# Sums of the down weights formed in DRAM by accumulating transfers, and four more lower parts prepared ahead, in a one-layer transformer kernel

## The chip, the cores and the metric

The kernel runs on one core of a Trainium2 chip. The metric is device microseconds (us) of that core for one execution, lower is better. Engines are named as the profile names them: PE (matrix multiply), DVE (vector), ACT (scalar activation), POOL (GpSimd), SP (the queue that issues nearly all transfers).

## What is computed

One layer on 512 rows of 1024 floats, all in float32: a gated feed-forward part, a mixer with two kinds of attention, and a second feed-forward part, each between two norms.

```python
def swiglu(h, w_gate, w_up, w_down):
    return (jax.nn.silu(h @ w_gate) * (h @ w_up)) @ w_down
...
h = swiglu(rms_norm(x, ff1_norm_pre[l]), ff1_w_gate[l], ff1_w_up[l], ff1_w_down[l])
x = x + 0.5 * rms_norm(h, ff1_norm_post[l])
h = hybrid_mixer(rms_norm(x, mix_norm_pre[l]), w_in[l], ...)      # diff attention and sparse attention
x = x + rms_norm(h, mix_norm_post[l])
h = swiglu(rms_norm(x, ff2_norm_pre[l]), ff2_w_gate[l], ff2_w_up[l], ff2_w_down[l])
x = x + 0.5 * rms_norm(h, ff2_norm_post[l])
```

The gate and up weights are 1024 x 2816, the down weights 2816 x 1024, `w_in` is 1024 x 2840.

## The kernel before, in words

**Precision.** A float32 product is made of three PE products of a shorter float type: each operand is split into an upper part (a cast, by ACT or DVE) and a lower part (the operand minus its upper part, by DVE), and PE adds upper x upper, upper x lower and lower x upper. So every weight tile that PE reads costs one cast and one DVE subtraction (`split`, L398 to L412; L404 is the cast, L407 the subtraction).

**Fewer products.** The products of both feed-forward parts are 2 x 2 block products made with seven block products in place of eight, numbered `m` = 1 to 7. Four of the seven use sums of weight blocks. In the gate and up half (names `ff1q..`, `ff1a`, `ff1b`, `ff1c`, line L664 on PE) these sums are DVE additions (L525). The quads `c` = 0 to 10 of gate (`e` = 0) and up (`e` = 1) weights come in two transfers each (`j` = 0, 1) of 512 KB, written (c, e, j) here; even c go through 4 `raw` tiles, odd c through 5 others (L332 issues them).

**The down half** (`ff1y`, L808 and L768 on PE) runs after it. `down_products` walks `m` in the order 1, 5, 6, 2, 7, 4, 3. `factor` (called for each m) fetches, for each of four row groups q, the weight blocks into `raw` tiles (`rawff1d`), adds them on DVE where m wants a sum (`add`, L601), and splits the result into `ff1dw<m><q>h` and `ff1dw<m><q>l`. For m = 5 the sum is block 00 + block 01, for 6 that sum + block 11, for 4 again that sum + block 10, for 7 block 01 + block 11. The activations' side is split likewise into `ff1dl`. The second feed-forward part does the same under `ff2` names.

**Lower parts ahead.** Twelve of the 512 KB pieces of `w_in` (three groups of columns, from 512, 0 and 1024) have their lower parts made early: `ahead` loads a piece (`pre`), casts it on ACT (L352), subtracts on DVE (L353) and stores the lower part to DRAM (`low`, L354); the projection later loads it instead of subtracting (L380). The four pieces of the columns from 1536 (`wp22` to `wp25`, the queries `qn`) are split when they are used.

**What sets the order.** Every step is recorded as an `Op` with a guessed cost and put in order by a planner (`Graph.order`), which simulates the engines with room in the tile pools (`ROOM`, `CAPS`) and picks on each engine the ready step with the highest level plus a number from the table `BIAS`. Each engine then runs its list strictly in that order. All transfers but a few are in SP's one list: an SP entry that waits holds back every transfer behind it.

Of the kernel before, what the change touches and what calls it, by code (L numbers as in the profile page):

```python
# [18 lines left out]
P = 128  # L19
# [34 lines left out]
    "ACT:fh>fdl": 5.6, "ACT:fh>fdl@ACT": -68.3, "ACT:fh>fdl@DVE": -0.3, "ACT:fh>fhh": 16.2, "ACT:fh>fhh@DVE": -182,
    "ACT:fhr>fhh": -138.7, "ACT:fhr>fhh@ACT": 20, "ACT:fhr>fhh@DVE": -242.2, "ACT:fp_>fp_": 134.6,
    "ACT:fqu>fqw": 937.3, "ACT:fqv>fqw": 100.3, "ACT:fy>fdp": 44, "ACT:gr>gh": 1255.8, "ACT:htk>hTk": -17.2,
    "ACT:htv>hTv": -173.1, "ACT:k__t>kT": 25.7, "ACT:ls>ls": 40.7, "ACT:n_nm>n_l": 46.2, "ACT:n_t>n_th": 116.1,
    "ACT:n_t>xa": -94.5, "ACT:n_t>xaf0": -210.9, "ACT:n_t>xaf1": 11.9, "ACT:n_t>xb": 327.4, "ACT:n_t>xc": 49.3,
    "ACT:n_t>xcf1": -137.4, "ACT:nc_pc>nc_pc": -84.3, "ACT:nc_t>nc_h": 25.6, "ACT:oN>oTn": 59.7,
    "ACT:oN>oTn@ACT": -12.7, "ACT:oN>oTn@DVE": -5.8, "ACT:pa>cd": 32.4, "ACT:pa>k__dup": 127.2, "ACT:pa>v": -109.4,  # L60
    "ACT:pb>k__dup": 21.1, "ACT:pb>v": 19.9, "ACT:pk>dkd": -48.9, "ACT:pre>pre": 191.7, "ACT:pre>preh": 0.9,
    "ACT:pv>dv": -90.4, "ACT:qTd_>qTd": 7.3, "ACT:qTn_>qTn": -44.2, "ACT:qd>qdd": 5.5, "ACT:qn>qdn": 23.6,
    "ACT:raw>wp": -2.3, "ACT:raw>wp@ACT": 20.1, "ACT:raw>wp@DVE": -4, "ACT:rawff1d>fdwh": 18.3,
    "ACT:rawff1d>fdwh@ACT": -113.1, "ACT:rawff1d>fdwh@DVE": -13.4, "ACT:rawff1q>fqw": 3.5, "ACT:rawff2d>fdwh": -25.9,
    "ACT:rawff2d>fdwh@ACT": -55.9, "ACT:rawff2d>fdwh@DVE": -67.9, "ACT:rawff2q>fqw": -83.9, "ACT:uk>uk": -98.6,
    "ACT:uv>uv": -22.7, "ACT:wrk>wk": 42.2, "ACT:wrv>wv": -96.2, "ACT:xaf0>xa": 12.9, "ACT:xaf0>xa@ACT": -0.2,
    "ACT:xaf0>xa@DVE": -99.7, "ACT:xaf1>xa": 5.7, "ACT:xaf1>xa@ACT": -49.8, "ACT:xaf1>xa@DVE": 21.3,
    "ACT:xcf0>xc": -165.4, "ACT:xcf0>xc@ACT": -92.6, "ACT:xcf1>xc": -156.2, "ACT:xcf1>xc@DVE": 213.5,
    "ACT:xi>n_ss": -6, "ACT:xj>n_ss": -11.3, "ACT:xm>n_ss": 95.1, "ACT:xrv>Xv": 189.3, "ACT:xrv>Xv@ACT": -72.1,
    "ACT:xrv>Xv@DVE": -45, "ACT:z>o_ss": 13.3, "DVE:acc>oN": -6, "DVE:cd_t>kc": 8, "DVE:ck>kcT": -19,  # L70
    "DVE:cmask>cmb": -77, "DVE:cmk>uk": -91.8, "DVE:cmv>uv": 103.6, "DVE:cv>vc": -15, "DVE:d>d_p": -21.7,
    "DVE:d_acc>o": 29.2, "DVE:d_r>d_p": 40.3, "DVE:d_t>d_th": 53.2, "DVE:dkt>dk": 7.8, "DVE:dl>d_r": -29.5,
    "DVE:dl>do_r": -0.4, "DVE:dmask>dmb": 5.2, "DVE:do_rr>o": 39.5, "DVE:do_t>oTd": 3.5, "DVE:fb>fhs": -65.9,
    "DVE:fb>fp_": 8.2, "DVE:fc>fhs": 24.7, "DVE:fc>fp_": 0.5, "DVE:fc__sg>fh": 23.8, "DVE:fd>fhs": -37.7,
    "DVE:fdp>fy": 12, "DVE:fdq>fy": 19.9, "DVE:fdr>fy": 1.9, "DVE:fds>fdl": 1.5, "DVE:fdu>fdwl": 62.2,
    "DVE:fh>fdl": -29.3, "DVE:fh>fds": 14.2, "DVE:fh>fh": 11.2, "DVE:fh>fhl": 92.5, "DVE:fh>fhl@DVE": 9.3,
    "DVE:fh>fhl@POOL": 1.1, "DVE:fhr>fhl": 156.6, "DVE:fp_>fh": 53.9, "DVE:fp_>fhs": 43.6, "DVE:fp_>fp_": 39.7,
    "DVE:fqu>fqw": 1255.3, "DVE:fqv>fqw": -218.6, "DVE:fy>fdr": 4.2, "DVE:gr>gh": 1080.8, "DVE:gsub>gsub": -24.1,
    "DVE:htk>hTk": -33.2, "DVE:htv>hTv": -60.3, "DVE:k__t>kT": 46.9, "DVE:lp>ls": 49, "DVE:ls>nlam": 0.6,
    "DVE:n>n_p": 4.9, "DVE:n_cf>n_p": 22, "DVE:n_cf>n_p@DVE": -1.2, "DVE:n_cf>n_p@POOL": 14, "DVE:n_l>n_cf": -8.8,  # L80
    "DVE:n_t>n_th": -9.5, "DVE:n_t>xa": -96.2, "DVE:n_t>xb": 0.5, "DVE:n_t>xc": 1861.1, "DVE:nc>nc_pc": -160.3,
    "DVE:nc_t>nc_h": -18.1, "DVE:oN>oTn@DVE": 0.7, "DVE:o_yg>xi": 22.6, "DVE:o_yg>xm": -74.8, "DVE:o_yg>xo": 136.3,
    "DVE:pa>k__dup": -42.2, "DVE:pb>k__dup": 6.6, "DVE:pb>v": 5.1, "DVE:pek>xrk": 235.1, "DVE:pev>xrv": 8.5,
# [1469 lines left out]
```

## Time and profile before

| | |
|---|---|
| runs | 999.89, 1001.97, 1004.66 us |
| median | 1001.97 us |
| the profiled execution | 1003.56 us, its span 1001.8 us |
| PE busy | 983.5 us (98%), DVE 882.9 us (88%), ACT 589.5 us (59%), POOL 32.3 us (3%) |
| bytes moved | 154.39 MB; the transfers of SP's queue take 45.4% of the 16 DMA engines' time |

Stages on the time axis of the profiled span: start and first norm to about 30 us, gate and up of the first part to 242 us, its down half to about 360 us, projections and compression to 425 us, attention to 590 us, output projection to 655 us, gate and up of the second part to 885 us, its down half to the end. A matmul that waits inside PE's pipeline is still counted as busy, so the count of matmuls in a stretch says more than the busy share.

### The profile page before, as it was taken

How to read it: one execution, taken by the hardware profiler on the slowest of the kernel's cores; microseconds unless marked ns; L12 is line 12 of the kernel's file. 1: busy time of each engine (PE TensorE's matmuls, PEld its weight loads, DVE VectorE, ACT ScalarE, POOL GpSimd, SP SyncE). 2: the span in 40 equal slices, each digit the busy share in tenths (PEclk: the TensorE clock that was granted, in tenths of full speed). 3: DMA queues.
4: the chain of work that ended last, by engine and by line, in shares of the span. 5: the costliest groups of instructions: out<-in, count | busy, mean ns of one | idle time of the engine just before them, and what ended most of it. 6: DMA issues, size and time to landing. Idle time of an engine off the chain costs nothing.

```text
span 1001.8 us, 17153 instructions
## 1 busy us (share of the span) xinstructions
PE 983.5 (98%) x6504; PEld 893.9 (89%) x6504; DVE 882.9 (88%) x1612; ACT 589.5 (59%) x1143; POOL 32.3 (3%) x68
## 2 busy tenths in 40 slices
PE   8999999999899999999999999999999999999997
PEld 7999999999688888888888888899999999988786
DVE  7999999999999687977887799899989998999984
ACT  8655555665454475577877677776554555545542
POOL 1000000000000030000000001310000000000001
PEclk9999999999899999999999999999999999999999
DMA  9126554556768754540403142361334231287752
GB/s 336 64 86 179 168 178 127 164 173 242 258 222 293 244 179 147 190 168 1 169 1 110 59 167 86 106 232 53 137 106 135 68 136 43 86 281 244 231 210 84
DMA packets 100420, 154.39 MB, mean 154 GB/s; under 512 B 11121, under 2 KB 61553, under 8 KB 100338
## 3 DMA queue, kind: packets, MB, share of 16 engines
q1 hardware_dynamic: 100338, 153.30, 45.4%
q8 instruction: 51, 0.84, 0.3%
q14 instruction: 31, 0.25, 0.1%
HBM read 137.55 MB, written 15.73 MB: 153 GB/s over the span
## 4 chain that ended last, share of the span: by engine, by line
PE 85%; DVE 6%; DMA 4%; ACT 2%; issue 1%; SPq 0%; POOL 0%; DVEq 0%; POOLq 0%; ACTq 0%
PE ff2b L664 9%; PE ff1b L664 9%; PE ff1y L808 7%; PE ff2c L664 6%; PE ff1c L664 6%; PE ff2a L664 6%; PE ff1a L664 6%; PE ff2y L808 5%; PE z L1410 4%; PE ff2y L768 3%; PE ff1y L768 2%; PE n_t L1306 2%; DMA rawff2d<-ff_w_down 1%; PE n L1190 1%; PE acc L398 1%
## 5 line engine op out<-in xcount | busy, mean ns | idle before, releaser
L1203 ACT ACTIVATE n_p<-n_p,n_nm 128x128 f32<-128x128 f32 (+3 forms) x64 | 35.3, 554 | 9.0 <-DVE n_nm L1201 8.6
L1201 DVE CUSTOM_DVE_ANT_0 n_p<-n,dmb 128x128 f32<-128x128 f32 (+3 forms) x64 | 28.3, 486 | 5.9 <-PE n L1191 5.6
L407 DVE TENSOR_TENSOR n_th<-n_t,n_th 128x512 fp32r<-128x512 f32 x40 | 25.8, 684 | 6.6 <-ACT n_th L404 6.4
L404 ACT CAST n_th<-n_t 128x512 fp32r<-128x512 f32 x40 | 21.6, 594 | 7.0 <-PE n_t L1306 6.7
L439 POOL TENSOR_SCALAR o_ms<-o_ss 128x1 f32<-128x1 f32 x12 | 4.0, 335 | 664.6 <-ACT junk L447 664.5
L691 ACT ACTIVATE ff1p<-ff1p 128x256 f32<-128x256 f32 x30 | 12.5, 418 | 19.2 <-DVE ff1p L703 19.2
L691 ACT ACTIVATE ff2p<-ff2p 128x256 f32<-128x256 f32 x30 | 12.5, 417 | 16.5 <-DVE ff2p L703 15.7
L1203 ACT ACTIVATE d_p<-d_p,d_nm 128x128 f32<-128x128 f32 (+3 forms) x32 | 17.7, 556 | 5.7 <-DVE d_nm L1201 5.5
L1306 PEld LDWEIGHTS n_t<-ident,n_p 128*128 128x128 f32 x160 | 18.6, 140 | 2.5
L1306 PE MATMUL n_t<-ident,n_p 128*128 128x128 f32 x160 | 20.7, 272 | 0.0
L703 DVE TENSOR_TENSOR ff2p<-ff2p,ff2b 128x512 f32<-128x512 f32 x30 | 20.4, 681 | 0.3 <-PE ff2b L664 0.3
L1190 PE MATMUL n<-kT,qTn 128*128 128x128 f32 (+3 forms) x64 | 20.4, 335 | 0.0
L703 DVE TENSOR_TENSOR ff1p<-ff1p,ff1b 128x512 f32<-128x512 f32 x30 | 20.4, 680 | 0.0
L1191 PE MATMUL n<-kT,qTn 128*128 128x128 f32 (+3 forms) x64 | 19.6, 321 | 0.0
L569 DVE TENSOR_TENSOR o_yg<-ff2y,g_ff_norm_post 128x512 f32<-128x512 f32 x8 | 5.5, 689 | 14.3 <-ACT junk L447 14.3
L447 ACT ACTIVATE junk<-ff2y 128x512 bf16<-128x512 f32 x8 | 4.8, 597 | 21.3 <-PE ff2y L768 21.3
L398 PE MATMUL acc<-n_th,v 128*64 128x512 f32 x40 | 16.1, 402 | 0.0
L1201 DVE CUSTOM_DVE_ANT_0 d_p<-d,dmb 128x128 f32<-128x128 f32 (+3 forms) x32 | 14.7, 486 | 1.2 <-PE d L1191 1.2
L399 PE MATMUL acc<-n_th,v 128*128 128x512 f32 x40 | 15.7, 393 | 0.0
L470 PE MATMUL n_t<-ident,n_xn 128*128 128x128 f32 x96 | 13.3, 286 | 1.2 <-DVE n_xn L463 1.2
L703 DVE TENSOR_TENSOR ff2p<-ff2c,ff2p 128x512 f32<-128x512 f32 x20 | 13.8, 688 | 0.3
L1296 DVE TENSOR_SCALAR n_p<-n_p,n_cf 128x128 f32<-128x128 f32 (+3 forms) x42 | 13.8, 380 | 0.3
(1831 smaller groups left out, 3562.6 us busy)
## 6 DMA issues: line engine op xcount, KB each, us to landing
rawff1d<-ff_w_down SPq DMA_DIRECT2D x36, 512.0 KB, 4.7
rawff2d<-ff_w_down SPq DMA_DIRECT2D x36, 512.0 KB, 5.0
rawff1q<-ff_w_gate SPq DMA_DIRECT2D x22, 512.0 KB, 5.8
rawff1q<-ff_w_up SPq DMA_DIRECT2D x22, 512.0 KB, 4.3
rawff2q<-ff_w_gate SPq DMA_DIRECT2D x22, 512.0 KB, 5.1
rawff2q<-ff_w_up SPq DMA_DIRECT2D x22, 512.0 KB, 4.2
raw<-w_in SPq DMA_DIRECT2D x20, 512.0 KB, 4.5
pre<-w_in SPq DMA_DIRECT2D x12, 512.0 KB, 4.2
```

The source lines that it names most:

```text
L398: nc.tensor.matmul(oh, vh, b(1), start=False, stop=False)
L407: V.tensor_sub(lo(), src(), f32(hi()))
L664: nc.tensor.matmul(o, T[k][:, s, i * P:(i + 1) * P], T[xm][:, r, i, :], start=start and e + i + s + r == 0, stop=stop and i == 3 and s == ...
L691: op("ACT", act(256), lambda: A.activation(T[sg][:, :256], T[sg][:, :256], AF.Silu), w=[sg])
L703: op("DVE", dve(512), lambda: fn(T[out], T[x], T[y]), r=[k for k in (x, y) if k != out], w=[out])
L768: nc.tensor.matmul(T[f"{f}y{t}{j}"], T[a[s]][:, sl], wp[i](r)[:, j, :], start=start and s + r == 0, stop=c == rest[-1] and s == 1, skip_gr ...
L808: nc.tensor.matmul(T[ys[u]], T[k][:, s, q % 2 * 2 + n, u * P:(u + 1) * P], T[ws[r]][:, n, :], start=m in (1, 5, 6) and q + n + s + r == 0, ...
L1190: nc.tensor.matmul(T[b][:, :L], qt[:, 0, h, :], k()[:, :L], start=True, stop=False)
L1201: op("DVE", dve(L), lambda: V.tensor_tensor_reduce(T[p][:, :L], T[b][:, :L], T["dmb"][:, S - L:], -1.0, 3e38, ALU.add, ALU.min, T[nm][:, 0 ...
L1203: op("ACT", act(L, 0.22), lambda: A.activation(T[p][:, :L], T[p][:, :L], AF.Exp, bias=T[nm][:, 0:1], scale=-1.0, accum_out=T[l][:, col:col ...
L1306: nc.tensor.transpose(T[bt][:, h * P:(h + 1) * P], T[p[h]][:, kb * P:(kb + 1) * P], ident)
L1410: nc.tensor.matmul(T[y[j]], T[f"oT{t}{'nd'[k < 4]}{s}"][:, k % 4, :], wp[wo[k]](r)[:, j, :], start=k == 4 and s + r == 0, stop=k == 3 and ...
```

## The change

It does four things.

1. `down_products` gets a second argument, the load after which it may begin (quad transfer 12, which is (3, 0, 0), of each part). For each q and each m of 5, 6, 7 and 4 it makes a 512 KB tile in DRAM (`ff1sum..`): SP copies one operand into it, DRAM to DRAM (L647 of the changed kernel), and POOL issues a transfer that adds the second operand onto it (L649). That is 16 copies and 16 accumulating transfers for each feed-forward part. The first operand of 6 is the finished sum 5, that of 4 the finished sum 6. POOL's sixteen stand in the order q by q, 5, 6, 7, 4.
2. `factor` now loads one `raw` tile for each m and q, from the weights or from the sum, and splits it. The 16 DVE additions of each part are gone, and the tiles `du` with them; 28 `rawff1d` loads stand where 36 stood.
3. The columns from 1536 join the pieces whose lower parts are made ahead: 16 in place of 12, with 1536 first.
4. `BIAS` is replaced by a longer table, entries of the form `...@engine` now count for every step, and the norm ahead of the first part has the names `na` (rows 0, 1) and `nb` (rows 2, 3).

```diff
-    "ACT:acc>ol": -8.4, "ACT:ck>kcT": 114.7, "ACT:cmk>prek": -4, "ACT:cmv>prev": -52.6, "ACT:cv>vc": -40.9,
...
+    "ACT:acc>ol": -15.1, "ACT:cd_t>kc@ACT": -26871.7, "ACT:ck>kcT": 75.7, "ACT:cmv>prev": -52.6,
...
-                    heapq.heappush(ready[e], (-o.level - (BIAS.get(f"{kind_of(o)}@{e}", 0.0) if len(o.eng) > 1 else 0.0), o.n, o))
+                    heapq.heappush(ready[e], (-o.level - BIAS.get(f"{kind_of(o)}@{e}", 0.0), o.n, o))
...
-    def down_products(f):
...
-        def add(dst, a, b, r):
-            op("DVE", dve(1024), lambda: V.tensor_add(T[dst], T[a], T[b]), r=[k for k in r if k != dst], w=[dst], port=True, chain="sum")
...
+    def down_products(f, after):
+
+
+        def src(q, kh, jh):
+            r0 = (2 * SPILL + 8 * kh + 2 * q) * P
+            return io[f"{f}_w_down"][0, r0:r0 + 2 * P, jh * 512:(jh + 1) * 512].rearrange("(k p) b -> p k b", p=P)
+
+        sums = {}
         for q in range(4):
-            new(f"{f}du{q}", ("M", "m_u"), [P, 1024])
+            for m, a, b in ((5, (0, 0), (0, 1)), (6, 5, (1, 1)), (7, (0, 1), (1, 1)), (4, 6, (1, 0))):
+                k = f"{f}sum{m}{q}"
+                d = sums[m, q] = dram.tile([P, 2, 512], F32, name=k)
+                first = sums[a, q] if isinstance(a, int) else src(q, *a)
+                op("SP", 1.46, lambda d=d, first=first: nc.sync.dma_start(d, first), r=[f"{f}sum{a}{q}"] if isinstance(a, int) else [],
+                   w=[k], after=after)
+                op("POOL", 7.0, lambda d=d, b=src(q, *b): nc.gpsimd.dma_start(d, b, accum_op=ALU.add), w=[k], after=after, chain="acc")
...
-    def factor(f, m, raw, add):
+    def factor(f, m, sums, src):
         for q in range(4):
-            u = f"{f}du{q}"
-            if m == 5:
-                a, b = raw(q, 0, 0, m), raw(q, 0, 1, m)
-                add(u, a, b, [a, b])
...
+            u = new(f"raw{f}d{m}{q}", "raw", [P, 1024])
+            part = {1: (0, 0), 2: (1, 0), 3: (1, 1)}.get(m)
+            a, r = (src(q, *part), []) if part else (sums[m, q], [f"{f}sum{m}{q}"])
+            v = lambda u=u: T[u].rearrange("p (a b) -> p a b", a=2)
+            pdma.append(op("SP", 1.46, lambda v=v, a=a: nc.sync.dma_start(v(), a), r=r, w=[u], chain="dma"))
...
-    dp1 = down_products("ff1")
+    dp1 = down_products("ff1", [qdma[12]])
...
-    low_i = {c: [ahead(*in_rows(c, 512, j)) for j in range(4)] for c in (512, 0, 1024)}
+    low_i = {c: [ahead(*in_rows(c, 512, j)) for j in range(4)] for c in (1536, 512, 0, 1024)}
...
-    w = in_pieces(1536, 512)
+    w = in_pieces(1536, 512, low_i[1536])
...
-    dp2 = down_products("ff2")
+    dp2 = down_products("ff2", [qdma[56]])
```

DVE at the start of the first down half, before: `ff1du` are the sums, `ff1dw5.`, `ff1dw6.` the split weights of m = 5 and 6, `ff1ds` and `ff1dl` the activations' side, `w2v` a small weight of the compression.

```order
L407 TENSOR_TENSOR ff1dw52l<-ff1du_3339,ff1dw52h 128x1024
L781 TENSOR_TENSOR ff1ds<-ff1ds,ff1h_1976 128x1024
...
L781 TENSOR_TENSOR ff1h_1976<-ff1h_1976 128x4x256
L781 TENSOR_TENSOR ff1ds<-ff1h_2491,ff1ds 128x1024
L353 TENSOR_TENSOR pre_2897<-pre_2897,pre8h 128x1024
L407 TENSOR_TENSOR w2v<-w2rv,w2v 128x128
L601 TENSOR_TENSOR ff1du_3427<-rawff1d_3321,rawff1d_3337 128x1024
L601 TENSOR_TENSOR ff1du_3273<-ff1du_3273,rawff1d_3359 128x1024
L601 TENSOR_TENSOR ff1du_3296<-ff1du_3296,rawff1d_3364 128x1024
L407 TENSOR_TENSOR ff1dw53l<-ff1du_3427,ff1dw53h 128x1024
```

The same place on DVE now:

```order
L450 TENSOR_TENSOR ff1dw52l<-rawff1d_3327,ff1dw52h 128x1024
L450 TENSOR_TENSOR ff1dl_3387<-ff1ds,ff1dl_3387 128x1024
L450 TENSOR_TENSOR ff1dw53l<-rawff1d_3370,ff1dw53h 128x1024
L726 TENSOR_TENSOR ff1h_3040<-ff1p_10_3185 128x256
L815 TENSOR_TENSOR ff1h_2040<-ff1h_2040 128x4x256
L450 TENSOR_TENSOR ff1dw60l<-rawff1d_3389,ff1dw60h 128x1024
L450 TENSOR_TENSOR ff1dw61l<-rawff1d_3395,ff1dw61h 128x1024
```

`ff1dw53l` has moved ahead of `w2v` and of two of the activations' steps, and no sum stands ahead of it. It is the 404th DVE row of the program before and the 392nd now.

SP in the gate and up half of the first part, before: entries 20 to 23, from (3, 1, 0) on.

```order
L332 DMA rawff1q_560<-ff_w_up 128x4x256
L332 DMA rawff1q_855<-ff_w_up 128x4x256
L332 DMA rawff1q_875<-ff_w_gate 128x4x256
L332 DMA rawff1q_897<-ff_w_gate 128x4x256
L695 DMA ff1hd_92<-ff1hs_511 128x1024
```

And now (`ff1sum_80` to `ff1sum_83` are the sums 5, 6, 7, 4 of q = 0, `ff1sum_84` to `ff1sum_87` those of q = 1):

```order
L375 DMA rawff1q_596<-ff_w_up 128x4x256
L647 DMA ff1sum_80<-ff_w_down 256x1x512
...
L647 DMA ff1sum_94<-ff_w_down 256x1x512
L647 DMA ff1sum_81<-ff1sum_80 16x8192
L647 DMA ff1sum_83<-ff1sum_81 16x8192
L375 DMA rawff1q_923<-ff_w_up 128x4x256
L375 DMA rawff1q_944<-ff_w_gate 128x4x256
L375 DMA rawff1q_964<-ff_w_gate 128x4x256
L729 DMA ff1hd_108<-ff1hs_529 128x1024
L375 DMA rawff1q_1162<-ff_w_up 128x4x256
L647 DMA ff1sum_85<-ff1sum_84 16x8192
```

Ten copies stand between (3, 1, 0) and (3, 1, 1): eight from the weights, and two that wait for accumulating transfers. Of the remaining six, `ff1sum_85` stands behind (4, 1, 0), `ff1sum_87` ahead of (5, 1, 1), `ff1sum_89` and `ff1sum_91` around (6, 1, 0) and (6, 1, 1), `ff1sum_93` behind (8, 0, 1), and the last, `ff1sum_95`, directly ahead of (8, 1, 0).

## Rows read from the trace of the kernel before

**Rows 1.** The page: busy time of each engine, share of the span, instructions.

```profile
PE 983.5 (98%) x6504; PEld 893.9 (89%) x6504; DVE 882.9 (88%) x1612; ACT 589.5 (59%) x1143; POOL 32.3 (3%) x68
```

**Rows 2.** Table by stretches; x counts instructions, then PE clock granted, DMA share.

```profile
core 0: us, PE busy (x) PEld busy (x) DVE busy (x) ACT busy (x) POOL busy (x), PEclk, DMA share, GB/s
75.00:250.00 175.00, 175.00 (x1432) 173.74 (x1431) 166.79 (x271) 98.68 (x168) 0.00 (x0) 1.00 0.55 175
250.00:275.00 25.00, 20.79 (x79) 16.40 (x78) 23.58 (x25) 11.08 (x15) 0.00 (x0) 0.86 0.78 260
...
300.00:325.00 25.00, 25.00 (x112) 20.71 (x111) 24.25 (x26) 11.70 (x13) 0.00 (x0) 1.00 0.89 297
...
425.00:650.00 225.00, 224.82 (x1297) 188.19 (x1295) 184.88 (x547) 165.25 (x420) 12.47 (x22) 1.00 0.27 97
675.00:875.00 200.00, 200.00 (x1669) 200.00 (x1669) 185.49 (x313) 106.98 (x193) 0.00 (x0) 1.00 0.29 96
...
925.00:950.00 25.00, 24.57 (x108) 19.60 (x107) 23.19 (x24) 13.55 (x15) 0.00 (x0) 1.00 0.72 232
```

**Rows 3.** The waits of PE, longest first: us in total, times, longest.

```profile
PE ff1y L808 <- ACT ff1dw53h L404: 2.4, 1, 2.4
PE ff1y L808 <- DVE ff1dw53l L407: 1.8, 1, 1.8
```

**Rows 4.** DVE in order of time from 259 us: start, duration, instruction, idle before.

```profile
259.75 1.22 DVE L353 TENSOR_TENSOR pre<-pre,pre8h 128x1024 fp32r<-128x1024 f32 x1
261.78 0.29 DVE L407 TENSOR_TENSOR w2v<-w2rv,w2v 128x128 fp32r<-128x128 f32 x1 [0.81 <-ACT w2v L404]
261.99 1.22 DVE L601 TENSOR_TENSOR ff1du<-rawff1d,rawff1d 128x1024 f32<-128x1024 f32 x1
263.12 2.35 DVE L601 TENSOR_TENSOR ff1du<-ff1du,rawff1d 128x1024 f32<-128x1024 f32 x2
265.40 1.22 DVE L407 TENSOR_TENSOR ff1dw53l<-ff1du,ff1dw53h 128x1024 fp32r<-128x1024 f32 x1
```

**Rows 5.** ACT in order of time, same stretch.

```profile
261.45 0.30 ACT L404 CAST w2v<-w2rv 128x128 fp32r<-128x128 f32 x1 [5.74 <-DMA w2rv<-cmp_v_w]
...
263.24 1.04 ACT L404 CAST ff1dw53h<-ff1du 128x1024 fp32r<-128x1024 f32 x1 [0.22 <-DVE ff1du L601]
```

**Rows 6.** The additions, line L601: count, shortest, median and longest ns, first to last.

```profile
L601 DVE TENSOR_TENSOR ff1du<-ff1du,rawff1d x8: 1215/1218/1226, 263.1 to 311.8; 128x1024 f32<-128x1024 f32 x8
...
L601 DVE TENSOR_TENSOR ff1du<-rawff1d,rawff1d x4: 1217/1220/1226, 243.9 to 262.0; 128x1024 f32<-128x1024 f32 x4
L601 DVE TENSOR_TENSOR rawff1d<-rawff1d,rawff1d x4: 1216/1221/1227, 283.7 to 297.0; 128x1024 f32<-128x1024 f32 x4
```

**Rows 7.** Transfers: the queue's packets, MB, share; issues with count, KB, us to landing.

```profile
q1 hardware_dynamic: 100338, 153.30, 45.4%
...
rawff1d<-ff_w_down SPq DMA_DIRECT2D x36, 512.0 KB, 4.7
...
low<-pre SPq DMA_DIRECT2D x12, 512.0 KB, 2.9
...
xo<-x SPq DMA_DIRECT2D x4, 512.0 KB, 9.6
...
w2rv<-cmp_v_w SPq DMA_DIRECT2D x1, 64.0 KB, 7.2
```

**Rows 8.** SP's transfers in order of time, gate and up half: start, us until issued.

```profile
29.03 24.98 SPq L332 DMA_DIRECT2D rawff1q<-ff_w_up  x2
...
155.29 1.57 SPq L332 DMA_DIRECT2D rawff1q<-ff_w_up  x2
```

**Rows 9.** First uses of (3, 1, 1) and of (8, 1, 0) on DVE.

```profile
69.49 0.69 DVE L525 TENSOR_TENSOR ff1q31u<-ff1q31u,rawff1q 128x512 f32<-128x512 f32 x1
...
159.71 0.68 DVE L525 TENSOR_TENSOR ff1q81u<-rawff1q 128x512 f32<-128x512 f32 x1
```

**Rows 10.** PE's first product with that sum of (8, 1, 0).

```profile
183.69 1.60 PE L664 MATMUL ff1c<-xa,ff1q81w 128*128 128x256 f32 x12
```

More of the change, by code (lines that the diff above doesn't have):

```diff
@@ L54 @@
[L54 to L83, printed above, removed]
@@ new lines @@
+    "ACT:oN>oTn@ACT": 4168.7, "ACT:oN>oTn@DVE": -5.8, "ACT:pa>cd": 33.4, "ACT:pa>cd@ACT": -121.4,
+    "ACT:pa>k__dup": 123.1, "ACT:pa>k__dup@ACT": -438.3, "ACT:pa>v": -110.3, "ACT:pa>v@ACT": 4321,
+    "ACT:pb>gates@ACT": 37696.8, "ACT:pb>k__dup": 21.1, "ACT:pb>k__dup@ACT": -43143.1, "ACT:pb>v@ACT": 166.8,
+    "ACT:pk>dkd": -789.1, "ACT:pre>pre": 191.7, "ACT:pre>preh": 0.9, "ACT:pv>dv": -90.4, "ACT:pv>dv@ACT": 527.6,
+    "ACT:qTd_>qTd": 7.3, "ACT:qTn_>qTn": -201.3, "ACT:qTn_>qTn@ACT": -49865.5, "ACT:qd>qdd": 5.5, "ACT:qn>qdn": 23.6,
@@ new lines @@
+    "ACT:raw>wp": 19.8, "ACT:raw>wp@ACT": 20.1, "ACT:raw>wp@DVE": -4, "ACT:rawff1d>fdwh": 21.5,
+    "ACT:rawff1d>fdwh@ACT": 9.4, "ACT:rawff1d>fdwh@DVE": -13.4, "ACT:rawff1q>fqw": 3.5, "ACT:rawff2d>fdwh": -25.6,
+    "ACT:rawff2d>fdwh@ACT": -55.9, "ACT:rawff2d>fdwh@DVE": -78.4, "ACT:rawff2q>fqw": -528, "ACT:uk>uk": -98.6,
+    "ACT:uk>uk@ACT": -224.4, "ACT:uv>uv": -26.9, "ACT:wrk>wk": 103.4, "ACT:wrk>wk@ACT": -6781.1, "ACT:wrv>wv": -96.2,
[3 rows of a table added]
+    "ACT:xi>na_ss@ACT": 52735.7, "ACT:xi>nb_ss": -6, "ACT:xj>n_ss": 31.3, "ACT:xj>na_ss": -11.3,
@@ new lines @@
+    "DVE:na_t>xb": 0.5, "DVE:na_t>xc": 1861.1, "DVE:nb_cf>nb_p": 22, "DVE:nb_cf>nb_p@DVE": -1.2,
+    "DVE:nb_cf>nb_p@POOL": 14, "DVE:nb_l>nb_cf": -8.8, "DVE:nb_t>nb_th": -9.5, "DVE:nb_t>xa": -85.1,
+    "DVE:nb_t>xa@DVE": 15683, "DVE:nb_t>xb": 0.5, "DVE:nb_t>xc": 1861.1, "DVE:nc>nc_pc": -160.3,
+    "DVE:nc_t>nc_h": -22.9, "DVE:oN>oTn@DVE": 0.7, "DVE:o_yg>xi": 22.6, "DVE:o_yg>xm": -35.9, "DVE:o_yg>xo": 136.3,
+    "DVE:pa>k__dup": 167.5, "DVE:pa>k__dup@DVE": -170.7, "DVE:pb>k__dup": 6.6, "DVE:pb>k__dup@DVE": 156.8,
@@ new lines @@
+    "DVE:pb>v": -27.5, "DVE:pb>v@DVE": 36.1, "DVE:pek>xrk": 235.1, "DVE:pev>xrv": 7.4, "DVE:pk>dkd": 204.5,
+    "DVE:pk>dkd@DVE": 208.5, "DVE:pre>pre": 222.3, "DVE:preh>pre": -570.4, "DVE:preh>pre@DVE": -820.8,
+    "DVE:prek>uk": 70, "DVE:prev>uv@DVE": -379.7, "DVE:pv>dv": -72.2, "DVE:pv>dv@DVE": -246.1, "DVE:qTd_>qTd": -43.3,
+    "DVE:qTn_>qTn": -40.5, "DVE:qd>qdd": -30.2, "DVE:qn>qdn": 81.3, "DVE:raw>wp": 8.8, "DVE:raw>wp@POOL": -7.8,
+    "DVE:rawff1d>fdu": -90.9, "DVE:rawff1d>fdwl": 0.3, "DVE:rawff1d>rawff1d": 13.9, "DVE:rawff1q>fqu": -811.2,
@@ new lines @@
+    "SP:g_ff1_norm_post>g_ff1_norm_post@SP": -1028, "SP:g_ff2_norm_post>g_ff2_norm_post": 27.9,
+    "SP:g_ff2_norm_pre>g_ff2_norm_pre": 284.4, "SP:g_mix_norm_post>g_mix_norm_post": -1.4,
+    "SP:g_mix_norm_pre>g_mix_norm_pre": 52, "SP:gr>gr": 2858.5, "SP:gr>gr@SP": 1334, "SP:gsub>gsub@SP": 5881.7,
+    "SP:lamt>lamt": 227.1, "SP:lamt>lamt@SP": 12778.2, "SP:low>wp@SP": -290.8, "SP:pek>pek": 4.5,
+    "SP:pek>pek@SP": 1359.1, "SP:pev>pev": -11, "SP:pre>low": -83.8, "SP:pre>low@SP": -637.3, "SP:pre>pre": 1574.1,
@@ L110 @@
+    "SP:xm>x": -6.1, "SP:xm>xm": -3.5,
 }
```

119 lines of the change are left out of this document (72 added, 47 removed), and 18 rows, old and new, of the table BIAS.

## The prediction

> **What bounds the kernel now.** I first read the page's busy times [rows 1]: PE is busy 98% of the span, DVE 88%. DVE's share says little by itself; what matters is where PE, the engine that sets the end, lacks work. For that I read the table by stretches [rows 2], counting matmuls and not busy time, since a matmul that waits in the pipeline counts as busy. In both gate and up halves PE runs at its pace: 1669 matmuls in 200 us are 120 ns each at a granted clock of 1.00, and the stretch from 75 us, whose last 8 us already hold longer matmuls, gives 122 ns. The down half's pace shows at 300 to 325: 112 matmuls in 25 us, 223 ns each. Against it 250 to 275 has 79, so 33 are missing, 33 x 0.223 = 7.4 us; and 925 to 950 has 108, so 4 x 0.223 = 0.9 us. So 8.3 us are all that the down halves can give back, however much DVE work goes away.
>
> What ends the wait in 250 to 275 I read in the list of PE's waits [rows 3], then in DVE's and ACT's instructions in order of time [rows 4, 5]. PE waits 2.4 us for `ff1dw53h` and 1.8 us for `ff1dw53l`, the last split of m = 5. ACT had stood 5.74 us on the small transfer `w2rv`, which takes 7.2 us to land although it is 64 KB [rows 5, 7]. DVE waits 0.81 us for ACT's cast of it, then makes the additions (261.99 and two from 263.12), which stand ahead of the split; ACT's cast starts when the sum is there, at 263.24, and DVE's subtraction at 265.40. The two waits make 4.2 us; the remaining 3.2 of the 7.4 I put down to the clock, whose mean in that stretch is 0.86, as against 1.00 at 300 to 325 [rows 2].
>
> **The change: what leaves the path.** 16 additions in each part leave DVE, 1.22 us each [rows 6]; neighbouring ones start about 1.14 us apart, so 2 x 16 x 1.14 = 36.5 us of DVE work. Nearly all of this lies beside PE's work and is worth nothing by itself. On the path are those ahead of `ff1dw53l`. It moves from DVE's row 404 to 392; six additions ahead of it are gone, 6 x 1.14 = 6.8 us, and `w2v` with its wait, another 1.1 us, now stands behind it. It would start at 265.40 - 6.8 = 258.6, or 257.5 with `w2v` gone, and end 1.2 us later. PE first stood there at 264.3 - 2.4 = 261.9 (264.3 is the end of the cast that starts at 263.24 and takes 1.04). That leaves 2.1 to 3.2 us to spare, and ACT's cast needs only a load now, not a sum. So both waits go, and with them the fall of the clock: **-7.4 us**. For 925 to 950 the list names no long wait; four of its additions too lie ahead of splits. It gives between 0 and 0.9; I take **-0.9**, because the same work leaves as in the first part.
>
> **What the four more lower parts cost.** Four subtractions of 1.22 us and four casts of 1.04 us [rows 4, 5] move from the projections into earlier stages, with four `pre` loads, four `low` stores and four loads of the stored parts. DVE has 175 - 166.8 = 8.2 us free at 75 to 250 and gains the additions' time in the down half, where the order puts most of the `pre` subtractions; ACT has 76 us free in the first stretch. So the moved work is covered. Without that cover it would cost 4 x 1.14 = 4.6 us of DVE. In the projections SP issues eight transfers for `qn` in place of four. PE's waits name none of `wp22` to `wp25` before, so there is no stall to remove and one to risk. Bounds -1 to +1; I take 0.
>
> **What the sums cost.** No accumulating transfer and no transfer started by POOL's queue stands in the trace, so both prices are bounds. First the room: 153.3 MB take 45.4% of 16 engines over 1001.8 us [rows 7], so 0.52 MB take 1.56 us of all sixteen. 16 copies cost 16 x 1.56 = 25 us, or twice that if reading and writing each count; an accumulation moves two reads and a write, 1.56 to 4.7 us, I take 3.1, or 50 us. That is 75 us for a part, 50 to 125. Free are 0.45 x 175 = 79 us at 75 to 250 and 0.71 x 200 = 142 us at 675 to 875 [rows 2]. It fits, tightly in the first part, and the down half itself, at 0.78 and 0.89 of the engines, loses 8 of 36 loads. At nothing, then, covered by PE's 120 ns stream.
>
> Second the order, since SP's list holds the waiting copies. For each q, sum 6 is copied from the finished sum 5 and sum 4 from the finished 6. With *a* for an accumulation from issue to landing and 4.7 us for a copy (a load of that size [rows 7]), one q takes 2a + 9.4 us, because POOL's list is q by q. Bounds for *a*: 2.9 us (a store) and 9.6 us (the slowest 512 KB transfer, `xo`); I take 4.7 + 2.9 = 7.6, a load and a store. The first copy can go when (3, 1, 0) has been issued at about 29.4 [rows 8] and lands at 34. The copy for sum 4 of q = 0, ahead of (3, 1, 1), is then free at 34 + 2 x 7.6 + 4.7 = 53.9; the same transfer was issued at about 53.7 before (the end of that row is 54.0), and is first used at 69.49 [rows 9]. The last copy, directly ahead of (8, 1, 0), is free at 34 + 3 x (2a + 9.4) + 2a + 4.7 = 66.9 + 8a, which is 127.7 at 7.6 and 143.7 at the upper bound; (8, 1, 0) was issued at 155.3 [rows 8]. So SP waits where it waited for a free `raw` tile anyway, and the sums are ready some 100 us before the down half. **0 us.**
>
> The sum: 1003.56 - 7.4 - 0.9 = 995.3 for the profiled execution. That execution lies 1.6 us above the median of the runs shown, so the median becomes 1001.97 - 8.3 = 993.7; I say 994.
>
> **Rivals.** (1) *The wait moves.* The 2.1 to 3.2 us of margin at `ff1dw53l` are small, and the loads that feed the splits come from one SP list behind the activations' `ff1hr` transfers; a load that lands that much later (against 4.7, `xo` shows 9.6) brings PE's stall back at m = 5 or at 6, with the clock's fall behind it. The next split stands right behind `ff1dw53l` on DVE, and four more `pre` subtractions fall into the same half. Then 5 to 7 of the 8.3 us are lost again: 999 to 1001. For it: the stretch keeps 0.78 to 0.89 of the DMA engines busy. Against: DVE has more room there than before.
>
> (2) *The accumulations are slow, and SP's list holds back the weights.* Here the time ends above that of before. DVE makes the sum of (8, 1, 0) at 159.71 and PE reads it at 183.69 [rows 9, 10], 24 us later. The last copy may come 24 us after 155.3, at 179.3 = 66.9 + 8a, before PE starves; that is **a = 14**. At a = 15.2, twice my value, it comes at 188.5, so PE stands 9 us in a part; taken the same in the second part, 18 - 8.3 gives +10 us, some 1012. At 20 us it is 47 us in a part, and about 1089 in all. For it: nothing like it was ever timed here, and sixteen run in a row. Against: 14 us is beyond every 512 KB transfer in the trace, the slowest at 9.6.
>
> [...]
>
> **How the numbers follow.** Forecast 0.60, rival 1 0.26, rival 2 0.14. A measurement of this kernel can tell about 0.5%, 5 us, from no change: faster is below 997, slower above 1007. The forecast lies in faster, rival 1 in the same, rival 2 in slower. The range: downward 993.7 less the 1 us of the lower parts and 2.4 for the spread of runs (half of 999.89 to 1004.66) is 990; upward rival 1 with its spread and a first part of late transfers, 1005. Left out are rival 2 and a little.
>
> **What would show it.** In the trace of after: no wait of PE for `ff1dw53`; some 112 matmuls and clock 1.00 in 250 to 275; DVE 36 us less busy; line L649 on POOL with a landing time near 7.6 us, surely below 14; SP's copies issued without pushing (3, 1, 1) past 69 us less its landing, or (8, 1, 0) past 179; 120 ns matmuls through both gate and up halves. I am wrong in the first step if PE's missing time is again in 250 to 300 under another name (rival 1), and in the last if the count of matmuls at 75 to 250 or 675 to 875 falls (rival 2).

## The result: 4% slower

The changed kernel takes 1041.1 us, the kernel before 1003.1 (medians of four runs each): 1.0373 times as long, interval 1.0332 to 1.0413. It is 47 us above the forecast of 994 and 36 above the upper end of the range. The outcome is the one that the prediction held for the least likely, rival 2. The landing time that it hung on had been taken nearly right; what was wrong is how many landings follow each other, and how much room PE had.

The profiled execution's span is 1034.7 us, 32.9 more than before. The page of after, as [rows 1]: busy time of each engine, and the two DMA queues (the second is POOL's) with packets, MB and share of the 16 engines.

```profile
PE 987.2 (95%) x6504; PEld 901.0 (87%) x6504; DVE 849.8 (82%) x1578; ACT 588.0 (57%) x1149; POOL 68.6 (7%) x100
...
q1 hardware_dynamic: 98994, 167.98, 48.0%
q0 software_dynamic: 8704, 16.78, 10.3%
```

DVE has 33 us less to do, as intended. The table by stretches answers [rows 2]; its columns are the same.

```profile
75.00:250.00 175.00, 152.53 (x1233) 151.84 (x1232) 140.99 (x240) 81.65 (x149) 12.58 (x12) 0.93 0.73 196
...
300.00:325.00 25.00, 25.00 (x112) 20.71 (x111) 23.10 (x23) 19.88 (x22) 0.00 (x0) 1.00 0.92 330
...
675.00:875.00 200.00, 187.01 (x1524) 186.43 (x1522) 169.43 (x288) 100.15 (x188) 19.20 (x20) 0.97 0.73 194
925.00:950.00 25.00, 25.00 (x112) 20.67 (x112) 22.88 (x23) 15.14 (x17) 0.00 (x0) 1.00 0.65 209
```

The down halves are mended: 112 matmuls in each 25 us, where 79 and 108 had stood. The loss is in both gate and up halves. At 120 ns, 175 us of them hold 1458 matmuls and 200 us hold 1669; 1233 and 1524 are there, so 225 x 0.12 = 27 us are missing in the first part and 145 x 0.12 = 17 in the second. 44 lost less 11 regained (the span of the run without the accumulations, below, is 990.6 us against 1001.8) is the 33 us of the span. PE's waits, as [rows 3], have new names (casts of gate and up weights of c = 8, 5, 4):

```profile
PE ff1b L698 <- ACT ff1q80w L587: 10.3, 1, 10.3
PE ff1b L698 <- ACT ff1q50w L587: 8.9, 1, 8.9
PE ff2b L698 <- ACT ff2q40w L587: 7.0, 1, 7.0
PE ff2b L698 <- ACT ff2q80w L587: 5.6, 1, 5.6
```

With two smaller ones (1.7 and 1.5) they make 35.0 us. The other 9 of the 44 go with the granted clock. In the 2.9 us behind the wait of 10.3 us it is 0.50 of full speed, and 12 matmuls take 2.90 us where the 12 ahead of the wait took 1.60. Counted over the 24 matmuls behind each of the four long waits, this costs 1.6, 2.4, 1.9 and 2.1 us, 8 in all.

How the longest wait comes about is seen in the chain that ended last, in order of time from 161 us (start, us, what). Read it downward: each line released the next.

```profile
161.47 6.46 DMA ff1sum<-ff_w_down
...
167.95 4.56 DMA ff1sum<-ff1sum
...
173.16 7.37 DMA ff1sum<-ff_w_down
180.54 0.02 issue
180.56 0.48 SPq L647
...
181.13 5.36 DMA rawff1q<-ff_w_up
...
186.51 0.69 DVE ff1q81u L568
...
194.53 0.63 ACT ff1q80w L587
...
195.17 5.03 PE ff1b L698 x22
```

An accumulation lands at 180.54, SP can issue the last copy, and only then (8, 1, 0), the entry behind it: at 181.13, where it was issued at 155.29 before [rows 8]. This is rival 2, link by link, up to the load.

The last link needs care. The profile puts PE's wait down to ACT's cast `ff1q80w`, which ended 0.02 us ahead of it, but the product that waits reads weights of c = 7. What it shares with DVE is its bank `ff1b`, in which PE adds up its products: DVE has to have read the one before (`ff1p<-ff1p,ff1b`), and this reading stands behind the sum `ff1q81u` in DVE's list. After:

```profile
194.34 0.68 DVE L737 TENSOR_TENSOR ff1p<-ff1p,ff1b 128x512 f32<-128x512 f32 x1
195.17 2.90 PE L698 MATMUL ff1b<-xa,ff1q70w 128*128 128x256 f32 x12 [10.31 <-ACT ff1q80w L587]
```

And the same two before, where PE does not wait:

```profile
168.65 0.68 DVE L703 TENSOR_TENSOR ff1p<-ff1p,ff1b 128x512 f32<-128x512 f32 x1
170.73 1.60 PE L664 MATMUL ff1b<-xa,ff1q70w 128*128 128x256 f32 x12
```

In all six waits that make the 35.0 us, PE's first weight load starts 0.11 to 0.12 us after such a reading ends, and in five of them slightly before the named cast is over. So a late load holds PE through DVE, which works through its list in order. Not every one of these loads is a weight. Ahead of the wait of 8.9 us (PE starts again at 118.99) DVE had stood on the lambda vectors, 32 KB each, which SP issued from 104.99 on, where it had been from 91.11 on before:

```profile
114.02 0.29 DVE L973 TENSOR_TENSOR lp<-lamt 128x128 f32<-128x128 f32 x1 [6.76 <-DMA lamt<-lambda_k]
```

What rival 2 had not foreseen is why the accumulations were so late. POOL's rows show it (start, duration, idle before and what ended it); they are sums 6, 7 and 4 of q = 0 and sum 5 of q = 1.

```profile
53.19 1.08 POOL L649 DMA_DIRECT2D ff1sum<-ff_w_down  x1 [15.19 <-DMA ff1sum<-ff1sum]
59.65 1.04 POOL L649 DMA_DIRECT2D ff1sum<-ff_w_down  x1 [5.38 <-issue]
69.28 1.05 POOL L649 DMA_DIRECT2D ff1sum<-ff_w_down  x1 [8.59 <-issue]
76.30 1.04 POOL L649 DMA_DIRECT2D ff1sum<-ff_w_down  x1 [5.97 <-issue]
```

Sum 7 needs nothing of sum 6, and sum 5 of the next q needs nothing of this one. Yet each starts 6 to 10 us after the one ahead of it, about when that one lands (the median landing is 8.2 us in the page's list of transfers). POOL counts as busy for 1 us only, and the wait is called "issue": it ends on nothing that the profile shows. Ten of the 16 accumulations of the first part wait so. One q then takes four landings, not two, and one copy, since the second copy is made beside sum 7.

### The profile page after: what moved, and what is told of

Same layout as the page of the kernel before. It is cut to its first block, busy times and chain, and to the rows that moved or that the text cites. A ratio compares the mean times of both kernels' runs of the same rounds, so it can differ in the third digit from the quotient of the medians.

```text
span 1034.7 us, 17249 instructions
## 1 busy us (share of the span) xinstructions
PE 987.2 (95%) x6504; PEld 901.0 (87%) x6504; DVE 849.8 (82%) x1578; ACT 588.0 (57%) x1149; POOL 68.6 (7%) x100
## 3 DMA queue, kind: packets, MB, share of 16 engines
q0 software_dynamic: 8704, 16.78, 10.3%
## 4 chain that ended last, share of the span: by engine, by line
PE 63%; DMA 18%; issue 9%; DVE 7%; ACT 2%; SPq 1%; POOL 1%; POOLq 0%; DVEq 0%; ACTq 0%
PE ff1y L842 7%; PE ff2y L842 7%; DMA ff2sum<-ff_w_down 6%; PE z L1445 4%; DMA ff1sum<-ff_w_down 4%; PE ff1b L698 3%; PE ff2b L698 3%; PE ff2y L802 3%; PE ff1y L802 3%; DMA ff2sum<-ff2sum 2%; PE ff1a L698 2%; PE ff2c L698 2%; PE ff2a L698 2%; PE ff1c L698 2%; PE n_t L1341 2%
## 5 line engine op out<-in xcount | busy, mean ns | idle before, releaser
L649 POOL DMA_DIRECT2D ff1sum<-ff_w_down x16 | 17.0, 1062 | 155.8 <-issue 81.3
L649 POOL DMA_DIRECT2D ff2sum<-ff_w_down x16 | 16.9, 1054 | 142.8 <-issue 81.7
L1333 ACT ACTIVATE n_p<-n_p,n_cf 128x384 f32<-128x384 f32 (+3 forms) x30 | 15.5, 560 | 1.5 <-DVE n_cf L1323 1.4
L698 PE MATMUL ff1b<-xa,ff1q70w 128*128 128x256 f32 x36 | 6.1, 331 | 10.3 <-ACT ff1q80w L587 10.3
```

Of the source, the lines that this page charges most:

```text
L649: op("POOL", 7.0, lambda d=d, b=src(q, *b): nc.gpsimd.dma_start(d, b, accum_op=ALU.add), w=[k], after=after, chain="acc")
L698: nc.tensor.matmul(o, T[k][:, s, i * P:(i + 1) * P], T[xm][:, r, i, :], start=start and e + i + s + r == 0, stop=stop and i == 3 and s == ...
```

## The experiments

### Room for POOL's transfers doubled

```
-    nc = bacc.Bacc("TRN2", ..., dynamic_dma_scratch_size=1024)
+    nc = bacc.Bacc("TRN2", ..., dynamic_dma_scratch_size=2048)
```

> One number changed: dynamic_dma_scratch_size, the kernel's setting for the room that POOL's transfers are written out in, is 2048 in place of 1024. In the changed kernel no accumulation starts before the one ahead of it has landed (7 to 13 us from one to the next), although the program has no such wait. Theory ring (POOL stands because that room holds one transfer): accumulations that wait for no copy now follow each other after 1 to 2 us, the waits of PE in both gate and up halves shrink or go, 995 to 1010 us. Theory single file (accumulations go one at a time by themselves) and theory traffic (the 33 MB more on the DMA engines delay the weights): no change, 1035 to 1042 us.

Measured: 1012.7 us, 1.0114 of before (1.0095 to 1.0132); about 28 of the 38 us are gone. POOL's rows in that run, from sums 6 and 7 of q = 0 on:

```profile
54.64 2.11 POOL L649 DMA_DIRECT2D ff1sum<-ff_w_down  x2 [16.04 <-DMA ff1sum<-ff1sum]
66.12 2.12 POOL L649 DMA_DIRECT2D ff1sum<-ff_w_down  x2 [9.37 <-DMA ff1sum<-ff1sum]
```

They now go in pairs, 1 us apart, and a pair waits for a transfer to land, never for "issue". That is the order that theory ring expected: one accumulation in flight at 1024, two at 2048. The two runs show no more of the setting than this, and "room" below means no more. Single file by itself and traffic alone fall. The time is 2.7 us above the range given: SP's list still waits for accumulations, and PE still waits 4.9, 2.9 and 2.8 us for c = 7, 6 and 5. The DVE work is the same: from 30 to 75 us DVE is busy 44.8 of 45 us, and the pair at 54.64 is issued in 2.11 us beside it, so here a busy DVE did not hold POOL's transfers back.

### The accumulations left out

```
-                op("POOL", 7.0, lambda ...: nc.gpsimd.dma_start(d, b, accum_op=ALU.add), ...)
+                op("POOL", 7.0, lambda: None, ...)
```

> Left out: the 32 accumulating transfers, so that the sums are plain copies of one operand; the order on every engine and all 32 copies are kept. Theories ring and single file: SP's copies wait for nothing but the copy before, PE's waits in the gate and up halves go, and what is left is the gain forecast in the down halves: 992 to 998 us. Theory traffic: half of the added traffic is still there, so about half of the loss too, 1012 to 1022 us.

Measured: 992.9 us, 0.9909 of before (0.9889 to 0.9929). Its stretches:

```profile
75.00:250.00 175.00, 175.00 (x1432) 173.75 (x1431) 165.56 (x271) 102.18 (x173) 0.00 (x0) 1.00 0.59 189
250.00:275.00 25.00, 25.00 (x112) 20.70 (x111) 23.95 (x24) 14.87 (x18) 0.00 (x0) 1.00 0.95 317
```

DVE reaches the split that PE had waited for at 254.7, where it had been 265.4 [rows 4]:

```profile
254.72 1.22 DVE L450 TENSOR_TENSOR ff1dw53l<-rawff1d,ff1dw53h 128x1024 fp32r<-128x1024 f32 x1
```

This is the forecast gain in size, 9.7 us where 8.3 was predicted, with 16 copies for each part still on the DMA engines, so no price of the copies shows. The whole loss hangs on the accumulations being there. The new table and the four lower parts are in this run too; no run has the table alone, so what it adds to the 9.7 us is not shown.

### The dependent copies issued by POOL

```
-   lambda d=d, first=first: nc.sync.dma_start(d, first)
+   lambda d=d, first=first, e=nc.gpsimd if isinstance(a, int) else nc.sync: e.dma_start(d, first)
```

> The eight copies of each part that wait for a finished sum are issued by POOL in place of SP; everything else stands as in the changed kernel. Theories ring and single file: nothing in SP's list waits for an accumulation any more, so the weights come in time and PE's waits in both gate and up halves go; POOL has 24 transfers one after another, 24 x 8 = some 190 us, so the last sums are ready at about 230 us, just before the down half: 993 to 1003 us. Theory traffic: the same bytes, 1035 to 1042 us.

Measured: 1002.2 us, 1.0001 of before (0.9987 to 1.0014). With the same bytes and the small room, all 38 us of the loss are gone once nothing in SP's list of the gate and up halves waits for POOL. Two things stand in its trace. First, a dependent copy does not wait for the accumulation ahead of it:

```profile
62.48 1.04 POOL L649 DMA_DIRECT2D ff1sum<-ff_w_down  x1 [6.79 <-issue]
63.03 1.00 POOL L647 DMA_DIRECT2D ff1sum<-ff1sum  x1
```

POOL's queue has 9216 packets here against 8704: 16 copies more, so 32 packets for a copy; an accumulation has 8704 / 32 = 272. So 272 + 32 packets are in flight together at 1024 (the copy at 63.03 starts 0.55 us behind the accumulation at 62.48), and in the changed kernel 272 + 272 were not (6 to 10 us apart). Second, 9.3 us remain against the run without accumulations; PE's one long wait in the gate and up half is 5.8 us, put down to `ff1q60w`, from 131 us on, and up to 11 us ahead of it ACT had stood on a `pre` load:

```profile
ACT pre0h L395 <- DMA pre<-w_in: 6.7, 1, 6.7
```

### The same transfers without the adding

```
-   nc.gpsimd.dma_start(d, b, accum_op=ALU.add)
+   nc.gpsimd.dma_start(d, b)
```

> Left out: the adding. POOL issues the same 32 transfers of the same shape as plain copies, so that a sum is its second operand alone; all else as in the changed kernel, room 1024. Theory ring: these transfers write out as many pieces as the adding ones, so they too start one at a time, each when the one before has landed; only the landing is shorter, so the time lies between: 1005 to 1030 us. Theory single file by the adding: plain transfers follow each other after 1 to 2 us, 992 to 1000 us.

Measured: 996.2 us, 0.9933 (0.9914 to 0.9953). Theory ring as it was put here is wrong in one point: a plain transfer has not as many packets as an adding one. POOL's queue and two of its rows:

```profile
q0 software_dynamic: 4608, 16.78, 5.3%
```

```profile
53.12 1.32 POOL L649 DMA_DIRECT2D ff1sum<-ff_w_down  x2 [14.04 <-DMA ff1sum<-ff1sum]
61.85 1.34 POOL L649 DMA_DIRECT2D ff1sum<-ff_w_down  x2 [7.41 <-DMA ff1sum<-ff1sum]
```

The same bytes make 144 packets for a transfer (4608 / 32, against 272), and two of those, 288, go in at once. By itself this run would fit "the adding makes them go singly" as well; with the doubled room, where two adding transfers go in at once, only a limit that goes with the setting fits both. If it goes by packets, an estimate from these counts puts it between 304 (272 + 32, in flight together) and 544 (272 + 272, not) at 1024.

### The order of the sums exchanged

```
-        for q in range(4):
-            for m, a, b in ((5, ...), (6, ...), (7, ...), (4, ...)):
+        for m, a, b in ((5, ...), (6, ...), (7, ...), (4, ...)):
+            for q in range(4):
```

> The two loops that make the sums are exchanged, nothing else: POOL's list is all four sums 5, then all 6, all 7, all 4, where it was 5, 6, 7, 4 for each q. The room is 1024 as in the changed kernel, so that accumulations still go one at a time, some 8 us each. A sum 5 that sum 6 is copied from is then finished four accumulations earlier than its copy's own addition, and the copies stand between nearly the same weight loads as before. Theory ring with SP's list behind it: the last copy is free at about 34 + 4.7 + 8 x 8 = 103 us in place of 181, PE's waits in the gate and up halves mostly go, 993 to 1005 us. Theory traffic: 1035 to 1042 us.

Measured: 1029.6 us, 1.0264 (1.0235 to 1.0293). The expectation missed. It followed the last copy alone, and the planner, which reckons 7.0 us for an accumulation and 2.0 for the landing of a copy, had now put the copies further ahead in SP's list:

```profile
67.76 8.77 SPq L647 DMA_DIRECT2D ff1sum<-ff1sum  x2
...
84.83 0.47 SPq L647 DMA_DIRECT2D ff1sum<-ff1sum  x1
85.39 1.08 SPq L375 DMA_DIRECT2D rawff1q<-ff_w_up  x2
```

The copy at 84.83 waits for the fifth accumulation, and (4, 1, 0) behind it goes at 85.39 in place of 73.4 in the changed kernel. PE waits 8.4 us for c = 4 and 7.6 us for c = 5 instead, and 9.9 us for c = 4 in the second part, although the last copy of the first part goes at 116.7. Each copy has to be followed, not the last one.

### Both cures together

> Both cures at once: the dependent copies on POOL, and the room 2048. Theory ring: POOL's chain is shorter, SP waits for nothing; what is left against the kernel without accumulations (992.9) is the traffic alone. If the stall of 5.9 us at 130 us in the run with the copies on POOL is traffic, it stays or grows: 1000 to 1006 us. If it came from POOL's single file, it goes: 993 to 996 us.

Measured: 1007.9 us, 1.0055 (1.0035 to 1.0075), slower than with the copies on POOL alone and 1.9 us above the range given. The stall at 110 to 140 us grew. In the profiled execution, at 1015.8 us the longest of the ten, PE waits 8.1 us, put down to `ff1q50w`, after DVE's 7.7 us wait in front of two small operations on the lambda vectors:

```profile
DVE lp L973 <- DMA lamt<-lambda_k: 7.7, 1, 7.7
```

POOL's last accumulation of the first part is issued at 171.15 in place of 189.64, so the same bytes are pressed into less time. That what is left after the order is mended is traffic, and that it bites where an engine's list stands on a small load that nobody needs soon, fits this, but it is argued from one trace.

### The small weight moved, on the kernel before

```
     order = g.order()
+    # casts of w2v, w2k and the subtraction for w2v: behind the split of ff1dw63
+    order = [o for o in order[:at + 1] if o not in late] + late + order[at + 1:]
```

> The kernel before with one thing moved: ACT's casts of w2v and w2k and DVE's subtraction for w2v stand behind the split of ff1dw63, where the changed kernel has them. No sums in DRAM, 16 additions on DVE in each part. If the 7.4 us missing in 250 to 275 come from ACT's wait for w2rv, as the prediction read them, nearly all of it comes back: 993 to 997 us for a kernel of 1002. If the additions on DVE ahead of the split are what holds PE, a stall of 2 to 4 us stays: 998 to 1001 us.

Measured: 1002.9 us, 0.9997 (0.9983 to 1.0011): nothing in the whole time. Both expectations missed. The first stretches and DVE in that run:

```profile
250.00:275.00 25.00, 21.90 (x95) 17.57 (x94) 24.93 (x27) 13.25 (x17) 0.00 (x0) 1.00 0.79 272
275.00:300.00 25.00, 23.98 (x104) 19.07 (x102) 22.05 (x23) 11.38 (x12) 0.00 (x0) 1.00 0.70 222
```

```profile
260.88 1.23 DVE L601 TENSOR_TENSOR ff1du<-rawff1d,rawff1d 128x1024 f32<-128x1024 f32 x1
262.02 2.35 DVE L601 TENSOR_TENSOR ff1du<-ff1du,rawff1d 128x1024 f32<-128x1024 f32 x2
264.29 1.22 DVE L407 TENSOR_TENSOR ff1dw53l<-ff1du,ff1dw53h 128x1024 fp32r<-128x1024 f32 x1
```

Without the wait for `w2rv` the split starts at 264.29 in place of 265.40 [rows 4]; the additions fill what ACT's wait had left. PE still waits 1.3 + 1.8 us there, with the additions ahead of the split. But 250 to 275 holds 95 matmuls where 79 had stood [rows 2], at a clock of 1.00 in place of 0.86: 16 of the 33 missing ones, 3.6 us, came back. They are lost again behind it, 8 of them in the next 25 us, and by 425 us PE is no further than before. So `w2rv` and the additions each held PE there, and with the additions still in DVE's list what the first gave back did not last.

### The four more lower parts alone, on the kernel before

```
-    low_i = {c: [...] for c in (512, 0, 1024)}
+    low_i = {c: [...] for c in (1536, 512, 0, 1024)}
...
-    w = in_pieces(1536, 512)
+    w = in_pieces(1536, 512, low_i[1536])
```

> The kernel before with one part of the change alone: the lower parts of the columns from 1536 are made ahead too, 16 pieces in place of 12; no sums in DRAM, the old table. The prediction put this at 0 with bounds of 1 us either way: 1000 to 1004 us. The rival: the moved subtractions meet the fullest stretches of DVE and cost 4 us or more, or they free the projections and give 3 us or more.

Measured: 1004.9 us, 1.0023 (1.0008 to 1.0037): 2.3 us slower (0.8 to 3.7), so most of the interval lies outside the bounds of 1. PE's waits name `k_dup` in the projections with 1.5 us, which those of the kernel before don't.

### Two sums of four in DRAM

```
-            for m, a, b in ((5, (0, 0), (0, 1)), (6, 5, (1, 1)), (7, (0, 1), (1, 1)), (4, 6, (1, 0))):
+            for m, a, b in ((5, (0, 0), (0, 1)), (7, (0, 1), (1, 1))):
...
+            if m in (6, 4):     # u is the tile with sum 5, b the raw block
+                op("DVE", dve(1024), lambda u=u, b=b: V.tensor_add(T[u], T[u], T[b]), ...)
```

> Of the four sums only 5 and 7 are made in DRAM, each from two blocks of weights: 8 copies and 8 accumulations in each part, half of the added traffic, and no copy that waits for an accumulation. The eight sums 6 and 4 are DVE additions again, onto the loaded sum 5. Theory ring with SP's list behind it: nothing in SP's list waits for POOL, so the gate and up halves run as in the kernel without accumulations; the additions that stood ahead of the split of ff1dw53 stand behind it: 992 to 997 us. If the traffic alone costs PE time, half of the 9 us between the run with the copies on POOL and the one without accumulations stays: 996 to 999 us. If the remaining additions hold PE at m = 6 or 4, a wait for ff1dw6 or ff1dw4 is named in the trace: 997 to 1001 us.

Measured: 1002.0 us, 0.9988 (0.9973 to 1.0002). This lies above all three ranges. Nothing in SP's list of the gate and up halves waits for POOL, and no `ff1dw` is among PE's waits, so the third theory lacks its sign. Half of the added bytes keep about as much of the loss as all of them had kept with the copies on POOL (1002.2), so the loss does not seem to go by the bytes alone; eight additions in each part are back on DVE here, and what they cost is not told apart. PE waits 4.1 us for `ff1q50w` in the profiled execution (1005.2 us, the longest of the twelve), and ahead of it DVE stands again on a small load:

```profile
DVE lp L977 <- DMA lamt<-lambda_k: 4.7, 1, 4.7
```

With 12 lower parts:

> The same with 12 lower parts made ahead, as in the kernel before. Alone on the kernel before the four more pieces cost 2.3 us (0.8 to 3.7). If they cost the same here, 1 to 3 us less than the run with two sums; if the new table, written for 16, has them well placed, 0 to 4 us more.

Measured: 1000.4 us, 0.9977 (0.9960 to 0.9994): 1.6 us less, about the price that the four pieces had on the kernel before, though the two intervals overlap.

### The small operations later in DVE's list

```
+    # lp and ls: twenty rows later on DVE
+    order = [o for o in order[:at + 1] if o not in small] + small + order[at + 1:]
```

> The run with two sums, with DVE's two small operations on the lambda vectors (lp, ls) twenty rows later in its list. In that run DVE stood 4.7 us on the load of these 32 KB vectors, issued at 100.6, and PE then waited 4.1 us for ff1q50w. Theory small loads (the added traffic makes small, unhurried loads land late, and an engine's list in order stands on them): that stall goes with its fall of the clock, 6 to 7 us less than the 1002.0 of two sums, 995 to 997 us. Theory weights late (the weight loads themselves come too late): the stall stays, 1000 to 1003 us.

Measured: 1000.3 us, 0.9965 (0.9948 to 0.9983). PE's wait for `ff1q50w` falls from 4.1 to 1.6 us, and the matmuls missing between 100 and 150 us from 55 to 25, 6.6 and 3.0 us. The direction is that of theory small loads, and the stall is halved, but the time fell by 1.8 us, with overlapping intervals, and not by 6 to 7. One reason stands in the trace: the next small operation in the list now stands on its load.

```profile
108.64 0.23 DVE L969 TENSOR_SCALAR gsub<-gsub 128x128 f32<-128x128 f32 x1 [3.35 <-DMA gsub<-diff_subln]
```

> The same move in the run with two sums and 12 lower parts, whose DVE wait for the lambda vectors was 4.3 us and whose PE loss at 100 to 125 us was 3.7 us. Theory small loads: 996 to 998 us in place of 1000.4; theory weights late: 1000 to 1001 us.

Measured: 999.5 us, 0.9956 (0.9939 to 0.9974), between the two ranges. It is not told apart from the run without the move, but it is faster than both kernels, by 0.4% and 4%. Its stretches:

```profile
75.00:250.00 175.00, 172.74 (x1420) 171.59 (x1419) 164.35 (x270) 99.61 (x172) 3.14 (x3) 1.00 0.61 179
250.00:275.00 25.00, 25.00 (x112) 20.71 (x111) 24.97 (x24) 12.86 (x17) 0.00 (x0) 1.00 0.78 265
```

## Why the prediction was wrong

**The gain: right in size, half right in its cause.** 8.3 us were forecast, the run without accumulations gives 9.7 (7.1 to 11.1 by its interval). `ff1dw53l` starts at 254.7 there, where 257.5 was reckoned, and both stretches have their 112 matmuls. The stall was laid to ACT's wait for `w2rv` first, with the additions behind it. Moving `w2rv` alone brought 16 of the 33 missing matmuls back into the stretch and nothing in the whole time, so both held PE, and the gain came only with the additions gone. A wait named in the list can hide the next one, 1.1 us behind it.

**The bytes: right.** An accumulation was put at 3.1 us of all 16 engines. Between 30 and 240 us of the trace of after POOL's queue takes 24.8%:

```profile
q0 software_dynamic: 4352, 8.39, 24.8%
```

That is 0.248 x 210 / 16 = 3.3 us. A copy was put at 1.56; the run without accumulations has 57.2% on SP's queue in that stretch against 45.0 before, 0.122 x 210 / 16 = 1.6.

**The landing time: right.** 7.6 us were taken for *a*, 8.2 is the median.

**The step that failed: "one q takes 2a + 9.4 us, because POOL's list is q by q".** It let sum 7 run beside sum 6, and the next sum 5 beside sum 4, since nothing in the program orders them. With the room of 1024 they do not overlap, and one q takes four landings and one copy, 4a + 4.7, since sum 7 covers the second copy. The last copy is then free at 34 + 3 x (4a + 4.7) + 2a + 4.7 = 52.8 + 14a, where the prediction had 66.9 + 8a: 14 landings follow each other in place of 8. At 8.2 this gives 167.6, and the trace has 180.56. The rest is that the first accumulation started at 36.76 and not at 34, and that the 14 steps took 8.9 us on average: the first took 11.8, and one waited for a copy that SP issued only at 103.80, behind other entries of its list. The prediction's own limit of 179.3 is then reached at a = 9.0, inside its own bounds of 2.9 to 9.6, and not at 14. The formula was carried to its limit for a slow *a*, up to 20 us, and never for transfers that queue behind each other, although the prediction itself said that nothing like them stood in the trace.

**The second step that failed: "24 us later".** The limit took the time from DVE's sum of (8, 1, 0) to PE's product with it as room. But PE needs the reading of `ff1b` that stands behind this sum in DVE's list. In the trace of after DVE's sum is 26.8 us later than before (186.51 against 159.71), PE's product ahead of the wait 14.0 us later (183.26 against 169.29), and PE waits 10.3 us, so 26.8 - 14.0 - 10.3 = 2.5 us were to spare and not 24. By an estimate from these rows (8, 1, 0) had to go by 155.3 + 2.5 = 157.8; 52.8 + 14a reaches that at a = 7.5, just below the 7.6 that was taken. With both steps mended the prediction's own *a* lands at the limit, so rival 2 would have had a chance near even and not 0.14.

**Only the last copy was weighed.** The price of rival 2 was 8a beyond one point, (8, 1, 0). PE waited at c = 5, 6, 7 and 8 in turn, and the clock fell with the long waits (0.83 and 0.84 of full speed at 100 to 130 and 160 to 200 us, 1.00 at 130 to 160). With the room doubled the last copy went at 169.8, ahead of 179.3, and still 1324 of 1458 matmuls stood in 75 to 250, 16 us lost. The run with the loops exchanged repeats the lesson: its last copy was early and the loss moved to c = 4.

**"The second part the same": too dear.** It lost 17 us against 27; the DMA engines had been busy 0.29 of the time there, against 0.55 [rows 2], which may be why; no run tried it.

**DVE's work and POOL's transfers.** With the room doubled and DVE busy for 44.8 of 45 us, two accumulations are issued in 2.11 us, so DVE's work is not what kept them apart in the changed kernel. What decided how many were in flight was the setting: one of 272 packets at 1024, two at 2048.

**The lower parts: most likely outside the bounds.** -1 to +1 was reckoned; alone on the kernel before they cost 2.3 us (0.8 to 3.7), and between the two runs with two sums 1.6 (these two intervals overlap). That they cost nothing in the changed kernel's own table is not shown.

**What stays open.** How much of the 9 us between the copies on POOL and the run without accumulations belongs to which load: the trace names one `pre` load there, and no run moved it; the run with two sums speaks against the bytes alone. And whether more than two accumulations go at once at 2048: in that run each pair waited for a transfer first.
